# Two of four weighted one-hots compared in one VectorE instruction and weighted by ScalarE, in the scatter of a PEER layer

## The chip, the cores and the metric

The kernel runs on one core of a Trainium2 chip. A core has five engines that run beside each other, each with its own in-order queue of instructions: TensorE (PE in the profile, with PEld for its weight loads), VectorE (DVE), ScalarE (ACT), GpSimd (POOL) and SyncE (SP, which here only issues DMAs). ACT and POOL also issue DMAs from their queues. Engines wait for each other by semaphores. The metric is the time of one execution on the device in microseconds (us).

## The reference

The program is one decoder block on 1024 tokens of width 1024: RMSNorm, two gated linear recurrences (HGRN2 and GLA), an output projection, and a PEER layer, then a last RMSNorm. Only the PEER layer is touched here:

```python
q = (xb @ w_q).reshape(PEER_BLOCK, PEER_HEADS, 2, PEER_HALF)
s = jnp.einsum('thpd,hpnd->thpn', q, sub_keys)
s_top, i_top = lax.top_k(s, PEER_TOPK)
...
expert = jnp.take_along_axis(cand_idx, pos, axis=-1)
g = jax.nn.softmax(best, axis=-1)
act = jax.nn.gelu(jnp.einsum('td,thkd->thk', xb, u[expert]), approximate=False)
return jnp.einsum('thk,thkd->td', (g * act).astype(xb.dtype), v[expert])
```

Each token picks 8 x 16 = 128 experts out of 16384, numbered i * 128 + j, with a weight g each. Each expert is a row of u and a row of v.

## The kernel before

The tokens are eight tiles of 128. Two tiles (0 and 1) are done by gathering: for each of the 128 picks one indirect DMA on the POOL queue fetches a row of u (or v) per token, 512 KB in all, into a buffer `g_row`, and one VectorE instruction takes the dot product (line 833) or adds the weighted row (line 835). A third tile, tile 2, is mixed: its dot products come from gathered rows of u, its sums over v from the dense form below. The other five tiles are dense: all 128 groups of 128 experts (a group is one j) are multiplied with the tokens by TensorE. Such a dense product for one j (`DenseProducts`) loads 512 KB of u, splits it into a high and a low part (`uh` by ScalarE, `ul` by VectorE, line 84), and issues 48 matmuls 128x128 by 128x320 into `hps`. 48 is two halves of the tokens, by eight slices, by the three terms of `mm3`.

For the dense form the weights of each token have to stand at their experts' places. That is the scatter (`scatter_dense`, lines 909 to 965). For a token it makes two one-hot matrices of 128 picks by 128: `oi` for i, and `oj` for j with the weight g in the place of the one. TensorE multiplies them (`tp`, line 923), which gives the token's 128 x 128 matrix of weights, and ScalarE copies it out (`ot`, line 924). A step does four tokens, a tile has 32 steps, and six tiles give 192 steps. The buffers `oi` and `oj` hold five steps (`lag + 1`), and the matmuls of a step are issued three steps after its one-hots. The finished `ot` is stored to `gd` in DRAM by DMAs of 512 KB.

Around the scatter a planner (`Weave`) decides the order. Each piece of work says how much of each engine it takes (`Work(pe=..., dve=..., span=...)`); the planner adds these up, takes the largest sum as the time that has gone by, and whenever a filler fits under it, emits the filler. Fillers are the dense products (pe 7.2, so one for each 7.2 us of time that TensorE has not been given) and the gathered rows. The order within an engine is then settled by a scheduler. Before the sixth tile of the scatter (tile 2, the mixed one) the planner emits all gathered rows of u for that tile that are still due (`finish_mixed`); they are called the row stage below.

A dense product made in or before the scatter is spilled: its result goes to `hd` in DRAM in two stores of 160 KB (lines 884, 885) and comes back late. After the scatter four more are emitted (`EXTRA`), and one more if their number is odd. What is left is made in `experts`. In its first part (`head`, `fresh`, the head below) each j costs a dense product and the 36 matmuls 128x128 by 128x512 into `sum` and `op` that add the experts' rows of v for the six tiles. In its second part (`tail`, `stored`, the tail below) the spilled products are read back, and each j costs only the 36 matmuls. The 512 gathered rows of tiles 0 and 1 run beside these two parts, one for each 2.75 us of planned time in the head and one for each 3.75 us in the tail; what is left of them after the last j is emitted at the very end (`weave.finish(rows)`).

Of the kernel before, what the change touches and what calls it, by code (L numbers as in the profile page):

```python
# [12 lines left out]
AF = mybir.ActivationFunctionType  # L13
OP = mybir.AluOpType
# [894 lines left out]
def scatter_dense(tc, con, wk, ps, e, weights, tiles, gd, nob, lag, before, first):  # L909

    nc = tc.nc
    iota = con["iota"].unsqueeze(1).to_broadcast([P, 4, P])
    steps = TB // 4

    def cols(t, t0):
        return t[:, t0:t0 + 4].unsqueeze(2).to_broadcast([P, 4, P])

    def place(c, tb, t4, ot, oi, oj):  # L920
        pt = ps.tile([P, 4, P], F32, name="tp")
        for q in range(4):
            nc.tensor.matmul(pt[:, q], oi[:, q], oj[:, q], start=True, stop=True)  # L923
        nc.scalar.activation(ot[:, :, t4 * 4:t4 * 4 + 4], pt.rearrange("p t j -> p j t"), AF.Copy)
        if t4 == steps - 1:
            dst = gd[:, (c - NG) * (P // TB) + tb]
            q0 = first() // 16 * 16 if c == tiles[-1] and tb else 0
            for q in range(q0, q0 + P, 16):
                out.append((dst[:, q % P:q % P + 16], ot[:, q % P:q % P + 16]))

    ahead, out = [], []
    for c in tiles:
        before(c)
        ints = wk.tile([P, 2, P], I32, name="ints", bufs=1)
        nc.vector.tensor_scalar(ints[:, 0], e[:, c], 7, None, OP.arith_shift_right)
        nc.vector.tensor_scalar(ints[:, 1], e[:, c], 127, None, OP.bitwise_and)
        fl = wk.tile([P, 2, P], F32, name="fl", bufs=1)
        nc.vector.tensor_copy(fl, ints)
        tp = ps.tile([P, 4, P], F32, name="tp")
        for q, src in enumerate((fl[:, 0], fl[:, 1], weights[:, c])):  # L940
            nc.tensor.transpose(tp[:, q], src, con["ident"])
        sm = wk.tile([P, 3, P], F32, name="sm", bufs=1)
        nc.scalar.activation(sm, tp[:, 0:3], AF.Copy)
        for tb in range(P // TB):
            ot = wk.tile([P, P, TB], F32, name="ot", bufs=nob)
            for t4 in range(steps):
                t0 = tb * TB + t4 * 4
                oi = wk.tile([P, 4, P], F32, name="oi", bufs=lag + 1)
                nc.vector.tensor_tensor(oi, iota, cols(sm[:, 0], t0), OP.is_equal)
                oj = wk.tile([P, 4, P], F32, name="oj", bufs=lag + 1)  # L950
                for q in range(4):
                    t = slice(t0 + q, t0 + q + 1)
                    nc.vector.tensor_scalar(oj[:, q], con["iota"], sm[:, 1, t], sm[:, 2, t], OP.is_equal, OP.mult)  # L953
                ahead.append((c, tb, t4, ot, oi, oj))
                if len(ahead) == lag:
                    place(*ahead.pop(0))
                if out:
                    nc.scalar.dma_start(*out.pop(0))
                if c == tiles[-1] and t0 == P - 4:
                    for late in ahead:  # L960
                        place(*late)
                yield Work(pe=0.9, dve=1.35, dma=0.7, span=1.7)
    for part in out:
        nc.sync.dma_start(*part)
        yield Work(dma=1.5, span=2)
# [182 lines left out]
def block_kernel(tc, a, out):  # L1148
    nc = tc.nc
    with ExitStack() as ctx:  # L1150
# [101 lines left out]
        with ExitStack() as c1:  # L1252
            weave.run(scatter_dense(tc, con, left(c1, "sa_wk", 2), left(c1, "sa_ps", 4, space=PSUM),
                                    e, g, [*range(NG + 1, 8), NG], gd, 2, 4,
                                    lambda c: rows.finish_mixed() if c == NG else None,
                                    lambda: dense.todo[0] + EXTRA))
# [38 lines left out]
```

## Time and profile before

| | |
|---|---|
| median of 3 runs | 3400.36 us (3396.97 to 3403.42) |
| the profiled execution, its own time | 3386.81 us |
| its span, first to last instruction | 3384.8 us |
| granted TensorE clock, mean | 0.967 of full speed |
| busy: PE, DVE, POOL, ACT | 92%, 77%, 32%, 29% |
| the scatter's 192 steps on DVE | 1346.0 to 1736.3 us |

The profiled execution is 13.6 us (0.4%) faster than the median of the runs shown, so a sum made in the trace gives a difference, and this is added to the median. Matmuls are pipelined, and a busy PE is not a PE at its peak: where it matters, count the matmuls in a stretch and multiply by the distance of their starts. The same holds for the other engines: two instructions of DVE overlap by some 0.08 us, so the distance of their starts is what a step costs.

### The profile page before, as it was taken

The numbers are of one execution on the slowest core, as the hardware profiler recorded it, in microseconds if no ns is written. First come the engines' busy times: TensorE is split into PE (matmuls) and PEld (weight loads), VectorE is DVE, ScalarE is ACT, GpSimd is POOL, SyncE is SP. The second block draws the span as 40 slices with busy tenths as digits, with TensorE's granted clock in tenths as the row PEclk, the third lists the DMA queues.
The fourth block names the chain that finished last, engine by engine and source line by source line (L and its number), as shares of the span: only waits on it lengthen the run. The fifth ranks groups of instructions, "written<-read, shape, count | busy, mean of one in ns | idle before, by whom it ended". The sixth has DMA issues, their size and how long they took to land.

```text
span 3384.8 us, 47850 instructions
## 1 busy us (share of the span) xinstructions
PE 3116.0 (92%) x18146; PEld 2763.2 (82%) x18146; DVE 2598.8 (77%) x5459; ACT 977.3 (29%) x1414; POOL 1083.7 (32%) x894
## 2 busy tenths in 40 slices
PE   8988986899689998999889999999999999999996
PEld 8976776777577988999888888888888887788885
DVE  4266499848676898999777777777878877778887
ACT  4233323233232222444232222222222222233231
POOL 2001133313355243000314444444444443322322
PEclk9999997999899999999999999999999999999998
DMA  5301533334697434455858888888888788988885
GB/s 171 126 16 59 188 130 125 103 130 152 231 331 300 143 112 141 165 207 207 312 202 291 279 268 282 272 272 278 277 277 280 265 270 268 325 287 280 284 282 172
DMA packets 348392, 741.49 MB, mean 219 GB/s; under 512 B 23409, under 2 KB 195330, under 8 KB 347906
## 3 DMA queue, kind: packets, MB, share of 16 engines
q0 software_dynamic: 94464, 343.97, 29.3%
q1 hardware_dynamic: 220866, 318.82, 29.2%
q10 hardware_dynamic: 32832, 75.64, 5.8%
q8 instruction: 142, 2.33, 0.3%
q14 instruction: 88, 0.72, 0.1%
HBM read 636.50 MB, written 101.84 MB: 218 GB/s over the span
## 4 chain that ended last, share of the span: by engine, by line
PE 34%; DVE 18%; DMA 12%; issue 5%; POOL 2%; ACT 2%; SPq 0%; ACTq 0%; DVEq 0%; POOLq 0%
DMA raw<-in_c_u_t 5%; PE hps L94 4%; PE tp L923 4%; PE hps L95 4%; PE hps L96 4%; PE op L94 4%; PE op L96 3%; PE op L95 3%; DVE g_acc L835 3%; DVE g_row L833 2%; DMA raw<-hd 2%; PE sum L94 2%; PE sum L96 2%; DVE ul L84 2%; PE sum L95 2%
## 5 line engine op out<-in xcount | busy, mean ns | idle before, releaser
L801 POOL DMA_INDIRECT g_row<-in_c_u_rows,e x384 | 497.0, 1294 | 984.2 <-DVE g_row L833 837.7
L96 PE MATMUL hps<-hnTh,ul 128*128 128x320 f32 x2048 | 646.6, 316 | 25.6 <-DVE ul L84 25.6
L94 PE MATMUL hps<-hnTh,uh 128*128 128x320 f32 x2048 | 650.3, 318 | 17.0 <-ACT ht L1012 12.6
L95 PE MATMUL hps<-hnTl,uh 128*128 128x320 f32 x2048 | 645.7, 315 | 3.7 <-DVE hnTl L84 3.7
L833 DVE SCALAR_TENSOR_TENSOR g_row<-g_row,g_hn 128x1024 f32<-128x1024 f32 x384 | 463.9, 1228 | 45.4 <-DMA g_row<-in_c_u_rows,e 40.1
L801 POOL DMA_INDIRECT g_row<-in_c_v_rows,e x256 | 321.2, 1255 | 528.5 <-DVE g_acc L835 466.4
L94 PEld LDWEIGHTS hps<-hnTh,uh 128*128 128x128 f32 x2048 | 391.8, 191 | 37.4 <-ACT ht L1012 25.3
L96 PEld LDWEIGHTS hps<-hnTh,ul 128*128 128x128 f32 x2048 | 391.6, 191 | 32.8 <-DVE ul L84 28.4
L95 PEld LDWEIGHTS hps<-hnTl,uh 128*128 128x128 f32 x2048 | 391.8, 191 | 9.8 <-DVE hnTl L84 4.1
L94 PE MATMUL op<-vh,wh 128*128 128x512 f32 x768 | 307.1, 400 | 35.0 <-DVE acc L1054 34.5
L835 DVE SCALAR_TENSOR_TENSOR g_acc<-g_row,g,g_acc 128x1024 f32<-128x1024 f32 x256 | 327.7, 1280 | 8.2 <-DMA g_row<-in_c_v_rows,e 4.0
L1054 DVE TENSOR_TENSOR acc<-op,acc 128x512 f32<-128x512 f32 x330 | 225.6, 686 | 116.2 <-PE op L96 108.0
L96 PE MATMUL op<-vh,wl 128*128 128x512 f32 x768 | 303.4, 395 | 0.0
L95 PE MATMUL op<-vl,wh 128*128 128x512 f32 x768 | 302.3, 394 | 0.0
L96 PE MATMUL sum<-vh,wl 128*128 128x512 f32 x768 | 300.5, 392 | 1.2 <-DVE wl L84 1.2
L94 PE MATMUL sum<-vh,wh 128*128 128x512 f32 x768 | 299.9, 390 | 0.9 <-ACT wh L83 0.9
L95 PE MATMUL sum<-vl,wh 128*128 128x512 f32 x768 | 299.8, 390 | 0.0
L84 DVE TENSOR_TENSOR ul<-raw,uh 128x1024 fp32r<-128x1024 f32 x128 | 168.1, 1314 | 145.2 <-ACT uh L83 145.2
L83 ACT ACTIVATE uh<-raw 128x1024 fp32r<-128x1024 f32 x128 | 135.5, 1059 | 409.3 <-PE hps L95 201.2
L923 PE MATMUL tp<-oj,oi 128*128 128x128 f32 x1536 | 211.5, 278 | 4.4 <-DVE oj L953 4.2
L953 DVE TENSOR_SCALAR oj<-iota,sm 128x128 f32<-128x128 f32 x768 | 212.7, 338 | 0.0
L94 PEld LDWEIGHTS op<-vh,wh 128*128 128x128 f32 x768 | 144.9, 189 | 78.3 <-DVE acc L1054 50.8
(241 smaller groups left out, 6125.6 us busy)
## 6 DMA issues: line engine op xcount, KB each, us to landing
raw<-in_c_u_t SPq DMA_DIRECT2D x128, 512.0 KB
raw<-in_c_v_rows SPq DMA_DIRECT2D x128, 512.0 KB
gd<-ot ACTq DMA_DIRECT2D x88, 512.0 KB
w_raw<-in_w_in SPq DMA_DIRECT2D x28, 1024.0 KB
gt<-gd SPq DMA_DIRECT2D x37, 768.0 KB
gt<-gd SPq DMA_DIRECT2D x18, 1152.0 KB
hd<-ht ACTq DMA_DIRECT2D x116, 160.0 KB
raw<-hd SPq DMA_DIRECT2D x58, 320.0 KB
```

Source lines behind the costliest of these rows:

```text
L83: nc.scalar.activation(hi, src, AF.Copy)
L84: return nc.vector.tensor_sub(lo, src, hi.bitcast(F32))
L94: nc.tensor.matmul(out, l[0], r[0], start=start, stop=False)
L95: nc.tensor.matmul(out, l[0], r[1], start=False, stop=False)
L96: nc.tensor.matmul(out, l[1], r[0], start=False, stop=stop)
L801: load = nc.gpsimd.indirect_dma_start(out=row, out_offset=None, in_=self.rows[kind], in_offset=bass.IndirectOffsetOnAxis(ap=self.e[:, c, s ...
L833: nc.vector.scalar_tensor_tensor(row, row, 1.0, self.hn, OP.mult, OP.mult, accum_out=act)
L835: nc.vector.scalar_tensor_tensor(self.acc, row, w, self.acc, OP.mult, OP.add)
L923: nc.tensor.matmul(pt[:, q], oi[:, q], oj[:, q], start=True, stop=True)
L953: nc.vector.tensor_scalar(oj[:, q], con["iota"], sm[:, 1, t], sm[:, 2, t], OP.is_equal, OP.mult)
L1054: last = nc.vector.tensor_add(acc[c][:, ds], op, acc[c][:, ds])
```

## The change

Of the four weighted one-hots of a step, the first two are compared in one VectorE instruction of 128x256 without a weight (line 951 of the new kernel), and ScalarE multiplies each of the two by its weight in place (line 955). The other two are made as before (line 957). The planner's numbers for a step are lowered with it.

```diff
                 oj = wk.tile([P, 4, P], F32, name="oj", bufs=lag + 1)
+                nc.vector.tensor_tensor(oj[:, :2], iota[:, :2], cols(sm[:, 1], t0)[:, :2], OP.is_equal)
                 for q in range(4):
                     t = slice(t0 + q, t0 + q + 1)
-                    nc.vector.tensor_scalar(oj[:, q], con["iota"], sm[:, 1, t], sm[:, 2, t], OP.is_equal, OP.mult)
+                    if q < 2:
+                        nc.scalar.activation(oj[:, q], oj[:, q], AF.Copy, scale=sm[:, 2, t])
+                    else:
+                        nc.vector.tensor_scalar(oj[:, q], con["iota"], sm[:, 1, t], sm[:, 2, t],
+                                                OP.is_equal, OP.mult)
...
-                yield Work(pe=0.9, dve=1.35, dma=0.7, span=1.7)
+                yield Work(pe=0.9, dve=1.15, dma=0.7, span=1.45)
```

The lowered numbers move work that the diff doesn't name. Three places show it. First VectorE's queue, two steps in the third tile of the scatter; `iota` is the row 0 to 127, `sm` holds the picks' i, j and g:

```order
L949 TENSOR_TENSOR oi<-iota,sm 128x512
L953 TENSOR_SCALAR oj<-iota,sm 128x128 x4
L949 TENSOR_TENSOR oi<-iota,sm 128x512
L953 TENSOR_SCALAR oj<-iota,sm 128x128 x4
L949 TENSOR_TENSOR oi<-iota,sm 128x512
```

And the same with the change:

```order
L949 TENSOR_TENSOR oi<-iota,sm 128x512
L951 TENSOR_TENSOR oj<-iota,sm 128x256
L957 TENSOR_SCALAR oj<-iota,sm 128x128 x2
L949 TENSOR_TENSOR oi<-iota,sm 128x512
L951 TENSOR_TENSOR oj<-iota,sm 128x256
L957 TENSOR_SCALAR oj<-iota,sm 128x128 x2
```

A step has four instructions on VectorE in place of five, and two more on ScalarE (384 in all), which in its queue stand between the copies of `ot`.

Second SyncE's queue from the last loads of the selection (`sc`) through the scatter; `in_c_u_t` is the source of the dense products, `gd` the store of the last `ot`, `in_c_v_rows` the first load of the head. Before:

```order
L646 DMA sc<-sc_d_65 128x1024
L859 DMA raw<-in_c_u_t 128x1024 x38
L795 DMA g_hn<-hn_dram 128x1024
L859 DMA raw<-in_c_u_t 128x1024
L964 DMA gd<-ot 128x1024 x8
L1008 DMA raw<-in_c_v_rows 128x1024
L859 DMA raw<-in_c_u_t 128x1024
```

And now:

```order
L646 DMA sc<-sc_d_65 128x1024
L859 DMA raw<-in_c_u_t 128x1024 x30
L795 DMA g_hn<-hn_dram 128x1024
L859 DMA raw<-in_c_u_t 128x1024 x2
L969 DMA gd<-ot 128x1024 x8
L859 DMA raw<-in_c_u_t 128x1024
L1013 DMA raw<-in_c_v_rows 128x1024
```

Fewer dense products stand in the scatter. Counted over the whole order, 116 stores into `hd` become 104, so 58 spilled products become 52 and the head has 76 in place of 70. Up to the last `tp` matmul of the first five tiles PE has 921 matmuls into `hps` within the scatter before and 645 now; behind the last `tp` of the scatter it has 3352 before and 3720 now. VectorE splits 17 `ul` in the first five tiles before and 11 now, 7 in the row stage before and 5 now.

Third VectorE's last instructions; `g_acc<-g_row` is a gathered row, `f_ms`, `g_hn` and `raw` with a buffer's number belong to the last norm of a tile; in the new order's rows `raw` is a buffer that a j of the tail is loaded into. Before:

```order
L835 SCALAR_TENSOR_TENSOR g_acc<-g_row,g,g_acc 128x1024
L1144 SCALAR_TENSOR_TENSOR raw_29177<-acc_16349,f_rs,nf 128x1024
L72 TENSOR_SCALAR f_ms<-ss 128x1
L835 SCALAR_TENSOR_TENSOR g_acc<-g_row,g,g_acc 128x1024
L1144 SCALAR_TENSOR_TENSOR raw_29205<-acc_16350,f_rs,nf 128x1024
L835 SCALAR_TENSOR_TENSOR g_acc<-g_row,g,g_acc 128x1024
L72 TENSOR_SCALAR f_ms<-ss 128x1
L1144 SCALAR_TENSOR_TENSOR g_hn<-g_acc,f_rs,g_row 128x1024
```

And now, the last gathered row and the norm of its tile:

```order
L835 SCALAR_TENSOR_TENSOR g_acc<-g_row,g,g_acc 128x1024
L84 TENSOR_TENSOR wl<-gt,wh 128x768
L1037 TENSOR_TENSOR gt<-raw_29012,gt 128x10x64
L84 TENSOR_TENSOR vl<-raw_29064,vh 128x1024
L72 TENSOR_SCALAR f_ms<-ss 128x1
L84 TENSOR_TENSOR wl<-gt,wh 128x768
L1149 SCALAR_TENSOR_TENSOR g_hn<-g_acc,f_rs,g_row 128x1024
```

The longer head takes in more gathered rows, and the last of them stands ahead of the splits (`vl`, `wl`) of three more j, where it was the last thing but the norm before.

## Rows read from the trace of the kernel before

**Rows 1.** Busy time of every engine in seven stretches of the span: start and end, length, then PE, PEld, DVE, ACT and POOL busy us with the number of instructions, the granted clock, the DMA share and GB/s.

```profile
1346.00:1628.00 282.00, 280.68 (x2169) 276.50 (x2170) 281.38 (x825) 125.38 (x217) 0.00 (x0) 0.99 0.52 190
1628.00:1684.00 56.00, 42.99 (x276) 42.33 (x275) 35.99 (x57) 14.06 (x22) 30.80 (x23) 0.89 0.93 354
1684.00:1738.00 54.00, 51.49 (x398) 50.30 (x398) 54.00 (x163) 22.90 (x40) 1.11 (x1) 0.99 0.38 148
1840.00:2490.00 650.00, 644.26 (x3494) 570.60 (x3493) 503.45 (x785) 152.34 (x208) 286.32 (x226) 1.00 0.83 276
2490.00:2790.00 300.00, 291.50 (x1578) 257.81 (x1577) 238.84 (x259) 70.02 (x95) 142.44 (x104) 1.00 0.82 271
2940.00:3340.00 400.00, 394.75 (x1714) 320.42 (x1713) 316.82 (x337) 116.76 (x140) 117.90 (x101) 1.00 0.83 273
3340.00:3384.00 44.00, 20.20 (x87) 15.72 (x85) 30.36 (x38) 7.94 (x14) 12.61 (x12) 0.78 0.48 167
```

**Rows 2.** The same stretches, PE's matmuls into `hps` (the dense products) alone: PE busy us and their number.

```profile
1346.00:1628.00 282.00, 174.31 (x901) 0.99 0.52 190
...
2490.00:2790.00 300.00, 143.27 (x898) 1.00 0.82 271
```

**Rows 3.** The same for PE's matmuls into `op` (first two rows) and into `sum` (last two), in the late head and in the tail.

```profile
2490.00:2790.00 300.00, 87.80 (x338) 1.00 0.82 271
2940.00:3340.00 400.00, 200.02 (x851) 1.00 0.83 273
...
2490.00:2790.00 300.00, 82.67 (x342) 1.00 0.82 271
2940.00:3340.00 400.00, 199.73 (x863) 1.00 0.83 273
```

**Rows 4.** Groups of instructions from 1340 to 1740 us (the scatter): line, engine, operation, out<-in, shape, count, then busy us and mean ns of one, then the engine's idle time before them and what ended it.

```profile
L953 DVE TENSOR_SCALAR oj<-iota,sm 128x128 f32<-128x128 f32 x768 | 212.7, 338 | 0.0
...
L949 DVE TENSOR_TENSOR oi<-iota,sm 128x512 f32<-128x512 f32 x192 | 130.9, 682 | 1.6 <-ACT sm L943 1.5
...
L84 DVE TENSOR_TENSOR ul<-raw,uh 128x1024 fp32r<-128x1024 f32 x28 | 34.0, 1217 | 12.9 <-ACT uh L83 12.9
L801 POOL DMA_INDIRECT g_row<-in_c_u_rows,e x23 | 31.9, 1388 | 315.8 <-DVE g_row L833 312.4 <-issue 3.4
...
L818 DVE TENSOR_TENSOR g<-g,act 128x128 f32<-128x128 f32 x1 | 0.3, 292 | 0.4 <-ACT act L817 0.4
```

**Rows 5.** DVE in order of time, one step and the start of the next: start, length, line, operation, shape, count.

```profile
1403.50 0.69 DVE L949 TENSOR_TENSOR oi<-iota,sm 128x512 f32<-128x512 f32 x1
1404.10 1.11 DVE L953 TENSOR_SCALAR oj<-iota,sm 128x128 f32<-128x128 f32 x4
1405.13 0.69 DVE L949 TENSOR_TENSOR oi<-iota,sm 128x512 f32<-128x512 f32 x1
```

**Rows 6.** PE in order of time: 32 matmuls of `tp` and the matmul into `hps` behind them, and two neighbours within a dense product.

```profile
1400.34 3.79 PE L923 MATMUL tp<-oj,oi 128*128 128x128 f32 x32
1403.89 0.39 PE L94 MATMUL hps<-hnTh,uh 128*128 128x320 f32 x1
...
1641.04 0.31 PE L95 MATMUL hps<-hnTl,uh 128*128 128x320 f32 x1
1641.19 0.31 PE L96 MATMUL hps<-hnTh,ul 128*128 128x320 f32 x1
```

**Rows 7.** DVE in order of time: the first gathered row behind the fifth tile, the first step of the sixth tile, and the one-hots of its last step.

```profile
1628.35 1.22 DVE L833 SCALAR_TENSOR_TENSOR g_row<-g_row,g_hn 128x1024 f32<-128x1024 f32 x1
...
1684.20 0.69 DVE L949 TENSOR_TENSOR oi<-iota,sm 128x512 f32<-128x512 f32 x1
...
1735.28 1.11 DVE L953 TENSOR_SCALAR oj<-iota,sm 128x128 f32<-128x128 f32 x4
```

**Rows 8.** ACT's groups from 1340 to 1740 us, columns as in rows 4.

```profile
L924 ACT ACTIVATE ot<-tp 128x512 f32<-128x512 f32 x192 | 114.2, 598 | 153.9 <-PE tp L923 147.1 <-DMA gd<-ot 2.3 <-issue 1.2
L83 ACT ACTIVATE uh<-raw 128x1024 fp32r<-128x1024 f32 x28 | 29.5, 1054 | 29.3 <-DMA raw<-in_c_u_t 14.6 <-PE hps L95 9.6 <-DVE oi L949 2.8
L884 ACT ACTIVATE ht<-hps 128x320 f32<-128x320 f32 x57 | 24.1, 435 | 55.6 <-DMA hd<-ht 26.6 <-PE hps L96 17.2 <-DMA gd<-ot 10.3
...
L817 ACT ACTIVATE act<-act 128x128 f32<-128x128 f32 x1 | 0.3, 309 | 1.3 <-DVE g_row L833 1.3
```

**Rows 9.** Just behind the scatter, SyncE's queue and PE in order of time; the bracket is the idle time ahead and what ended it.

```profile
1737.59 6.57 SPq L964 DMA_DIRECT2D gd<-ot  x8
...
1762.00 0.64 PE L94 MATMUL hps<-hnTh,uh 128*128 128x320 f32 x1 [11.26 <-ACT ht L1012]
```

**Rows 10.** The end of the program in order of time on PE, DVE, ACT and SyncE's queue.

```profile
3361.61 0.39 PE L96 MATMUL op<-vh,wl 128*128 128x512 f32 x1
...
3362.54 0.68 DVE L1054 TENSOR_TENSOR acc<-op,acc 128x512 f32<-128x512 f32 x1
...
3377.93 1.06 ACT L1142 ACTIVATE g_hn<-g_acc 128x1024 f32<-128x1024 f32 x1 [6.41 <-DVE g_acc L835]
...
3379.93 1.28 DVE L1144 SCALAR_TENSOR_TENSOR g_hn<-g_acc,f_rs,g_row 128x1024 f32<-128x1024 f32 x1 [0.66 <-POOL f_rs L74]
...
3381.24 0.33 SPq L1145 DMA_DIRECT2D out_dram<-g_hn  x1
```

## The prediction, made before the changed kernel ran

> **What bounds the kernel now.** I read the busy time by stretches first, because the change sits in one stage and the share of a whole span says nothing about it. In the first five tiles of the scatter VectorE is busy 281.4 of 282 us and PE 280.7 of 282: both are full [rows 1]. Then comes the row stage, 56 us in which PE is busy 43.0 at a granted clock of 0.89, with the DMA engines at 93%, and then the sixth tile, in which VectorE is busy 54.0 of 54. Behind it the head and the tail, where PE is busy 97 to 99% of the time.
>
> Then one step of the scatter in order of time: a step begins 1.63 us after the one before (1403.50 to 1405.13), 0.60 of it the `oi` compare and 1.03 the four one-hots of `oj`, 0.257 each [rows 5]. 160 steps make 260.8 us, and 17 `ul` splits at 1.14 (1.217 less the overlap of 0.08) make 19.4 [rows 1, 4]: 280 of the 282 us. PE's side of the same stretch: a dense matmul starts 0.147 us after the last, and 32 matmuls of `tp` take 3.55 [rows 6]. 901 dense matmuls [rows 2] are 132 us, the `tp` of 160 steps (eight each) 142, together 274. So PE has no more than 8 us to spare there: a shorter VectorE step is worth little unless PE is given less, and that is what the planner's lowered numbers do. This is the point on which the forecast turns: dense products leave the scatter and have to be paid for in the head.
>
> **The change part by part.**
>
> First five tiles. Two one-hots go, 2 x 0.257 = 0.514 us a step. The compare of 128x256 is in no row. The nearest two are operations on two tensors, one of 128x128 at 0.292 and the `oi` compare of 128x512 at 0.682 [rows 4]; between them on a line 256 columns give 0.42, or 0.34 from start to start. The lower end is 0.21 (a 128x128 one), the upper 0.60 (a 128x512 one); I take 0.34, the point between two rows of the same kind. A step is then 0.60 + 0.34 + 0.514 = 1.456 us. 160 of them are 233, 11 `ul` splits 12.5, five tile starts 3.5: 249 us for VectorE. PE has 645 dense matmuls, 94.5 us, and the 142 of `tp`: 237. VectorE is late by 12, and where the order lumps `tp` or dense matmuls, one of the two engines waits, since only five steps of buffers lie between them; I add 6. 282 becomes 255, a gain of 27 us (23 to 33).
>
> A rule of the Trainium skill speaks against this term. Its page VectorE: DVE Perf Modes, section Walkthrough: the 8-slice pipeline in each mode, says that an fp32 operation with one tensor and scalars can use both read ports and do two elements a cycle, and that one on two tensors cannot. By streaming alone, at its 0.96 GHz, the compare would cost an estimated 0.27 us and the two operations that it replaces 0.13, a step would grow by 0.13 and the term would be a loss of 21. Here rows decide otherwise: a one-hot takes 0.257 from start to start whatever its 128 columns cost, so most of it is a fixed cost, paid once less. The side of that rule is the last rival below.
>
> ScalarE gets the two weightings. The nearest row is a 128x128 ACTIVATE, 0.309 us [rows 8]. A step is then 0.598 + 2 x 0.309 = 1.22 us of ScalarE, and the 11 products' share (1.054 + 2 x 0.435 each) 0.13 more: 1.35, under the 1.456 of VectorE. So I price it at nothing, hidden beside VectorE; without that cover it costs what is worked out under the first rival. What is queued behind a waiting weighting on ScalarE is the copy of `ot` three steps older, and PE needs that for the fourth `tp` buffer; ScalarE's idle time today, 147 us in front of `ot` for PE [rows 8], is the room.
>
> Row stage. From the first gathered row to the next step of the scatter 55.9 us pass [rows 7]. It is DMA-bound: 354 GB/s for 56 us are 19.8 MB [rows 1]. Two products fewer fall in it (249 dense matmuls were there, 135 stand there now), 2.4 of them with 0.5 MB of u and 0.3 MB of `hd` each, so 2.0 MB less, 5.6 us at the same rate; two `ul` splits fewer, for which rows had to wait, 2 to 3 us more. I take 8 (4 to 14).
>
> Sixth tile. Its 32 steps run from 1684.20 to 1736.3 [rows 7], 52.1 us, all of it VectorE. The step shrinks as before, 32 x 0.173 = 5.5 us, but PE was busy 51.5 of 54 [rows 1] and has the same products there: 3 us (0 to 5).
>
> Head and tail. 52 products are spilled in place of 58, so six j move from the tail into the head. In the late head 898 dense matmuls are 18.7 products in 300 us [rows 2] and 680 adding matmuls 18.9 j [rows 3]: 15.95 us a j. In the tail 1714 in 400 us are 47.6 j: 8.40 [rows 3]. The six cost 6 x 7.55 = 45.3 us. PE's order has 368 dense matmuls more behind the scatter, 7.67 products; the other 1.67 are spilled ones that now come just behind it, 11.8 us of PE. There PE stands idle for 11.26 us while the stores of `gd` and the first loads of the head go through [rows 9], so they may be free. Bounds: 45 and 57; I take 50.
>
> End. The last matmul ends at 3362.0 and the program 22.8 us later, because gathered rows and their norm come last [rows 10]; in the last 44 us PE is busy for 20.2 [rows 1]. With three j still to split behind the last row that tail of rows goes, and the last norm is late next: an add (0.68), the square to the end of the program from 3377.93 on (6.9), some 0.2 between: 7.8 us. Gain 15 (12 to 17).
>
> Sum against the profiled execution: -27 - 8 - 3 + 50 - 15 = -3 us, 3384 in place of 3386.8. On the median of 3400.4 that is 3397. About 0.2%, 6.8 us, is what a measurement of this kernel can tell from no change, so the forecast is no change: VectorE's time saved is handed to TensorE's queue in the head.
>
> **The rivals.**
>
> Slower: ScalarE becomes the link that ends last. Its point is a step of ScalarE above 1.456 us. For it: a weighting cannot pass a `ht` copy that waits for a store of `hd` or for PE (26.6 and 17.2 us of such waits now [rows 8]), and the one-hots of a step now go VectorE, ScalarE, PE with five buffers. Against it: the 1.35 worked out above. At the old pace of 1.63 the five tiles gain only what fewer splits give, about 7, and the sixth nothing: -7 - 8 + 50 - 15 = +20, 3420; half of that effect is 3409. The Trainium skill, page ScalarE: Activation LUTs, section What ACT_TABLE_LOAD costs, adds weight to this rival: it gives 186 ns and 0.833 per column, and 93 ns more for an operand per partition, which the weight is. That is an estimated 0.386 us in place of 0.309, and a step of ScalarE of 1.50; no row here has a per-partition scale on so small a tile.
>
> Faster: the row stage falls to what POOL needs to issue. 23 gathers at 1.388 and 0.3 between them are 39 us [rows 4], 17 less than now, and the 1.67 products are wholly free: -27 - 17 - 3 + 45 - 15 = -17, 3383. For it: fewer stores compete. Against it: the 12 MB of gathered rows (23 of 512 KB) and the stores of `gd` stay.
>
> The end gives nothing: if the rows on the chip still lag behind their place in the order, since each waits for its DMA, the last 15 us stay: +12, 3412.
>
> The compare costs as much as a 128x512 one (0.60): the step is 1.72, nothing is gained on VectorE, and 160 steps cost 14 more than before: about +30, 3430.
>
> **How the numbers follow.** The forecast has 0.52, with its own range of 3387 to 3408; the ScalarE link 0.20, the faster row stage 0.17, the end without gain 0.08, the dear compare 0.03. Within the forecast a third of its chance lies below -6.8 and a tenth above +6.8: faster 0.16, same 0.30, slower 0.06. The row stage gives 0.16 to faster; the link 0.17 to slower and 0.03 to same; the end 0.06 to slower and 0.02 to same; the compare 0.03 to slower. Sums: faster 0.32, same 0.36, slower 0.32. The range leaves out the far ends of the link and of the row stage: 3381 to 3419.
>
> **What would show it.** VectorE's step at 1.45 us with the compare near 0.42; weightings near 0.31 or 0.39 on ScalarE; first five tiles near 255 us and PE idle some 15 us more in them; the row stage near 48; some 16 us a j in the head, 8.4 in the tail; the last norm within 9 us of the last matmul. Wrong if the five tiles stay near 275 us with PE or VectorE waiting for ScalarE, if head and tail cost under 40 us more, or if a gathered row is last again.

## The result and the profile after

The changed kernel takes 3438.32 us (median of 4 runs, 3428.97 to 3450.53), against 3398.66 for the kernel before beside it on the same chip: a ratio of 1.0114, with a 95% interval of 1.0096 to 1.0132. It is slower by some 39 us. The prediction was 3397, no change, with a range of 3381 to 3419: the time lies 19 us above the range.

The profiled execution after took 3450.53 us of its own (span 3448.6), 12 us over its median, and the one before 3386.81, about 12 under its own. Of the 64 us between the two traces only some 40 are the change, so each length below is checked against other executions.

First the busy time by stretches, columns as in [rows 1]: the five tiles, the row stage, the sixth tile, the early head and, last, the end.

```profile
1351.00:1643.00 292.00, 255.72 (x1898) 251.84 (x1898) 252.63 (x665) 200.16 (x513) 3.10 (x3) 0.93 0.45 168
1643.00:1693.00 50.00, 28.77 (x168) 27.06 (x168) 30.56 (x50) 13.71 (x25) 27.08 (x21) 0.80 0.98 380
1693.00:1743.00 50.00, 47.98 (x382) 47.47 (x381) 47.95 (x129) 36.48 (x95) 0.00 (x0) 1.00 0.34 130
1850.00:2500.00 650.00, 638.04 (x3435) 564.33 (x3434) 497.38 (x774) 150.29 (x205) 282.83 (x223) 0.99 0.82 272
...
3404.00:3448.00 44.00, 32.14 (x141) 25.95 (x139) 20.05 (x30) 6.79 (x12) 3.29 (x6) 0.91 0.22 84
```

The first row is where the forecast broke. It has 1898 of PE's matmuls where before had 2169, and VectorE's shorter steps, and is longer: 292 us in place of 282. Before, PE and VectorE were both full there [rows 1]; now PE is busy for 255.7 of 292 and VectorE for 252.6, PE's granted clock is 0.93 in place of 0.99, and ScalarE is at 200, not full either. Three engines with room and a stage that got longer means that they wait for each other in turn. Who waits for whom is in the groups of these 292 us, columns as in [rows 4]; PE, VectorE, ScalarE:

```profile
L923 PE MATMUL tp<-oj,oi 128*128 128x128 f32 x1248 | 172.1, 287 | 4.4 <-ACT oj L955 4.4
L96 PE MATMUL hps<-hnTh,ul 128*128 128x320 f32 x213 | 73.2, 349 | 31.5 <-DVE ul L84 31.5
...
L949 DVE TENSOR_TENSOR oi<-iota,sm 128x512 f32<-128x512 f32 x160 | 111.2, 695 | 35.4 <-PE tp L923 31.9 <-ACT sm L943 3.1
L957 DVE TENSOR_SCALAR oj<-iota,sm 128x128 f32<-128x128 f32 x318 | 96.5, 351 | 0.0
L951 DVE TENSOR_TENSOR oj<-iota,sm 128x256 f32<-128x256 f32 x160 | 68.3, 427 | 0.0
...
L955 ACT ACTIVATE oj<-oj,sm 128x128 f32<-128x128 f32 x318 | 109.3, 393 | 21.8 <-DVE oj L951 19.1 <-DVE oi L949 1.1 <-DVE oj L957 0.9
L924 ACT ACTIVATE ot<-tp 128x512 f32<-128x512 f32 x155 | 90.6, 586 | 69.9 <-PE tp L923 69.8
```

PE waits 31.5 us for `ul`, the low parts that VectorE splits off for the dense products, and VectorE waits 31.9 us for `tp`, that is for free buffers of `oi`. Neither wait was there before: there VectorE's `oi` compares waited 1.6 us in the whole scatter, nearly all of it for `sm` [rows 4], and PE's matmuls with `ul` not at all in the same five tiles:

```profile
L96 PE MATMUL hps<-hnTh,ul 128*128 128x320 f32 x300 | 97.6, 325 | 0.0
```

PE waits for a weighting (L955) for only 4.4 us, so ScalarE is not what it waits for. The compare is 0.43 and a weighting 0.39 us.

One of these waits in order of time, on PE, VectorE and ScalarE, at the end of the second tile:

```profile
1453.63 0.30 PE L95 MATMUL hps<-hnTl,uh 128*128 128x320 f32 x1
1457.87 0.64 PE L96 MATMUL hps<-hnTh,ul 128*128 128x320 f32 x1 [3.94 <-DVE ul L84]
1458.31 0.47 PE L94 MATMUL hps<-hnTh,uh 128*128 128x320 f32 x1
1458.58 0.47 PE L95 MATMUL hps<-hnTl,uh 128*128 128x320 f32 x1
...
1451.39 0.43 DVE L951 TENSOR_TENSOR oj<-iota,sm 128x256 f32<-128x256 f32 x1
1455.14 0.69 DVE L949 TENSOR_TENSOR oi<-iota,sm 128x512 f32<-128x512 f32 x1
1456.59 1.23 DVE L84 TENSOR_TENSOR ul<-raw,uh 128x1024 fp32r<-128x1024 f32 x1
1462.02 0.29 DVE L938 CAST fl<-ints 128x256 f32<-128x256 int32 x1 [4.20 <-PE tp L941]
...
1451.57 1.06 ACT L83 ACTIVATE uh<-raw 128x1024 fp32r<-128x1024 f32 x1
...
1454.92 0.68 ACT L955 ACTIVATE oj<-oj,sm 128x128 f32<-128x128 f32 x2
```

ScalarE has `uh` ready at 1452.6, but VectorE's in-order queue has more steps of the scatter in front of the split and comes to it only at 1456.59. PE has begun the product, needs `ul` for its matmuls of L96, and stands still for 3.94 us. VectorE waits 4.20 us in its turn: its next instruction belongs to the start of a tile (L938) and needs the one buffer `fl`, which PE's transposes (L941) free, and these stand behind the wait in PE's queue. At the next product, within a tile, it is the buffers of `oi` that it waits for, 3.71 us behind a wait of PE of 4.33 us:

```profile
1484.40 0.63 PE L96 MATMUL hps<-hnTh,ul 128*128 128x320 f32 x1 [4.33 <-DVE ul L84]
...
1488.06 0.69 DVE L949 TENSOR_TENSOR oi<-iota,sm 128x512 f32<-128x512 f32 x1 [3.71 <-PE tp L923]
```

PE pays twice, since two dense matmuls start 0.27 us apart behind the wait and not 0.147 [rows 6]. PE's busy time and granted clock before the wait, in it, behind it, and when it has recovered:

```profile
1444.00:1454.00 10.00, 9.94 (x84) 1.00 0.49 195
1454.00:1458.00 4.00, 0.13 (x1) 0.89 0.19 68
1458.00:1464.00 6.00, 6.00 (x26) 0.50 0.30 87
1464.00:1474.00 10.00, 10.00 (x81) 1.00 0.47 189
```

For 6 us the clock is 0.50, the 1.2 GHz level, behind some 4 us in which PE did next to nothing.

The order of the program says why the split is late. Counted over the whole order, set beside each product the number of steps that stand on VectorE ahead of its `ul`, and the number whose `tp` stand on PE ahead of its first matmul with `ul`. Before, 16 of the 17 splits of the first five tiles stand 4 to 11 steps ahead of their use and one stands 1 step behind it. After, 9 of 11 stand 2 to 5 steps behind it, and PE waits for a split nine times in these tiles (in all, times, longest, in us):

```profile
PE hps L96 <- DVE ul L84: 31.5, 9, 5.0
```

VectorE can be five steps ahead of PE at most, as there are five buffers, so a split 5 steps late is reached only when all of them are full. That is in the order and could have been counted before the run.

The end, which answers to [rows 10]: the last matmul and the last gathered row with its norm.

```profile
3436.39 0.39 PE L96 MATMUL op<-vh,wl 128*128 128x512 f32 x1
...
3374.66 1.28 DVE L835 SCALAR_TENSOR_TENSOR g_acc<-g_row,g,g_acc 128x1024 f32<-128x1024 f32 x1
3380.07 1.29 DVE L1149 SCALAR_TENSOR_TENSOR g_hn<-g_acc,f_rs,g_row 128x1024 f32<-128x1024 f32 x1 [0.46 <-POOL f_rs L74]
```

The gathered rows are done some 73 us before the program's end, and the last matmul ends 11.9 us before it, in place of 22.8.

### The profile page after: what moved, and what is told of

It is laid out like the page before. It is cut to its first block, busy times and chain, and to the rows that moved or that the text cites. A ratio compares the mean times of both kernels' runs of the same rounds, so it can differ in the third digit from the quotient of the medians.

```text
span 3448.6 us, 48207 instructions
## 1 busy us (share of the span) xinstructions
PE 3138.0 (91%) x18146; PEld 2783.0 (81%) x18146; DVE 2573.6 (75%) x5279; ACT 1081.7 (31%) x1792; POOL 1082.8 (31%) x894
## 4 chain that ended last, share of the span: by engine, by line
PE 29%; DVE 20%; DMA 11%; issue 9%; POOL 3%; ACT 2%; SPq 0%; DVEq 0%; POOLq 0%; ACTq 0%
DMA raw<-in_c_u_t 5%; DVE g_acc L835 4%; PE hps L94 4%; PE op L94 4%; PE hps L96 3%; PE hps L95 3%; PE op L96 3%; PE op L95 3%; DVE g_row L833 3%; PE tp L923 3%; POOL g_row L801 2%; DVE ul L84 2%; DVE acc L1059 2%; DMA raw<-hd 2%; PE sum L94 2%
## 5 line engine op out<-in xcount | busy, mean ns | idle before, releaser
L96 PE MATMUL hps<-hnTh,ul 128*128 128x320 f32 x2048 | 651.2, 319 | 51.9 <-DVE ul L84 51.9
L96 PEld LDWEIGHTS hps<-hnTh,ul 128*128 128x128 f32 x2048 | 394.7, 193 | 62.5 <-DVE ul L84 57.8
L94 PE MATMUL op<-vh,wh 128*128 128x512 f32 x768 | 307.4, 400 | 49.6 <-DVE acc L1059 49.2
L96 PE MATMUL op<-vh,wl 128*128 128x512 f32 x768 | 304.4, 396 | 0.0
L96 PE MATMUL sum<-vh,wl 128*128 128x512 f32 x768 | 301.3, 393 | 0.0
L83 ACT ACTIVATE uh<-raw 128x1024 fp32r<-128x1024 f32 x128 | 135.5, 1058 | 435.9 <-PE hps L95 254.2
L1017 ACT ACTIVATE ht<-hps 128x320 f32<-128x320 f32 x152 | 65.8, 433 | 472.3 <-PE hps L96 468.3
```

Source lines behind the costliest of these rows:

```text
L83: nc.scalar.activation(hi, src, AF.Copy)
L94: nc.tensor.matmul(out, l[0], r[0], start=start, stop=False)
L96: nc.tensor.matmul(out, l[1], r[0], start=False, stop=stop)
L1017: nc.scalar.activation(ht, hps, AF.Gelu)
```

## The experiments

Three theories stood at the start. **S**: late splits. **N**: the planner's lowered numbers, by giving PE slack and the head six more j. **L**: ScalarE's weightings as a link. The first four runs are a square: new or old instructions, new or old numbers, and the new instructions with a rule that brings the splits forward. Each ratio is to the kernel before, run beside it.

**New instructions, old numbers.**

```diff
-                yield Work(pe=0.9, dve=1.15, dma=0.7, span=1.45)
+                yield Work(pe=0.9, dve=1.35, dma=0.7, span=1.7)
```

> The new instructions with the planner's old numbers (1.35, 1.7), so again 58 spilled products and nothing moved into the head. Theory S (late splits: in the new order each split `ul` of a dense product stands on VectorE 3 to 5 steps behind the place at which PE asks for it, PE waits for it, its clock falls, VectorE then waits for PE): the order with these numbers still has 15 of 17 splits of the first five tiles behind PE's place, so these tiles take longer than before, 295 to 320 us against 282, with over 30 us of PE waiting for `ul`, and the time is 3405 to 3435. Theory N (the lowered numbers alone did it, by giving PE slack and the head six more j): the time is at or under that of before, 3385 to 3400. Theory L (ScalarE's weightings are a link that ends last at 1.8 us a step): first five tiles about 291 us as with the change, and with nothing moved into the head about 3408, PE waiting for ScalarE and not for `ul`.

3435.91 us (ratio 1.0106, 1.0076 to 1.0136). N fell as the whole cause: with the old numbers, and nothing moved into the head, it is as slow as the change. S has it nearly right: the first five tiles took 318.4 us, the time is 1 us above its range, and PE's wait is 26.6 us where over 30 were expected. Their stretch, and the waits in it:

```profile
1348.00:1665.00 317.00, 289.25 (x2167) 286.49 (x2168) 256.34 (x667) 209.58 (x528) 0.00 (x0) 0.95 0.45 166
...
L96 PE MATMUL hps<-hnTh,ul 128*128 128x320 f32 x297 | 97.8, 334 | 26.6 <-DVE ul L84 26.6
...
L949 DVE TENSOR_TENSOR oi<-iota,sm 128x512 f32<-128x512 f32 x160 | 110.0, 687 | 53.2 <-PE tp L923 49.7 <-ACT sm L943 3.5
```

In this order 14 of 17 splits are late by 1 to 5 steps. So it is the new instructions, not the numbers, with which the scheduler settled on late splits; why it places them so is not shown.

**Old instructions, new numbers.** The same line the other way round, in the kernel before.

> The old instructions with the planner's new numbers (1.15, 1.45), so 52 spilled products and six j more in the head, as with the change. S: the order has nearly all splits at or ahead of PE's place, so PE hardly waits for `ul` in the first five tiles, and VectorE is full: 160 steps of 1.63, 11 splits of 1.14 and 3.5 us of tile starts are 277 us; with the row stage at -6, the end at -15 and the head and tail at +50 to +65 the time is 3422 to 3440. N: first five tiles about 291 us with PE waiting for `ul` as with the change, 3438 to 3450. L: as S. What head and tail cost more than before is the price of the six j by itself.

3429.95 us (1.0096, 1.0058 to 1.0134), the first five tiles 274.6 us: VectorE full, as S and L had it. One split of 11 is late here.

```profile
1347.00:1621.00 274.00, 255.40 (x1929) 245.65 (x1929) 273.77 (x817) 117.16 (x202) 0.00 (x0) 0.99 0.48 179
...
L96 PE MATMUL hps<-hnTh,ul 128*128 128x320 f32 x218 | 71.6, 334 | 6.0 <-DVE ul L84 6.0
```

The numbers alone cost 32 us too, but elsewhere: from the end of the scatter to the last matmul this run takes 1695.8 us, against 1625.6 before. That is the price of the six j in the head and some of the difference between executions; the averages below part the two.

**The splits brought forward** to two steps behind the product's place in the program, in the changed kernel.

```diff
+            self.splits.append([2, self.options[0].last])
...
-                nc.vector.tensor_tensor(oi, iota, cols(sm[:, 0], t0), OP.is_equal)
+                cmp = nc.vector.tensor_tensor(oi, iota, cols(sm[:, 0], t0), OP.is_equal)
+                for late in [x for x in dense.splits if x[0] == 0]:
+                    tc.add_manual_dep(cmp.ins, late[1].ins.name, nosync(), reason="split first")
+                dense.splits = [[n - 1, x] for n, x in dense.splits if n]
```

> The changed kernel with one rule more for the order: VectorE's compare two steps behind a product's place in the program has to stand behind that product's split, so the splits stand 2 steps behind PE's place and not 4 or 5; nothing else is asked. S: PE's wait for `ul` in the first five tiles falls from 31.5 us to under 10, its clock is back at 0.97 or more there, these tiles take 255 to 268 us in place of 291, and the time is 3402 to 3416 against 3438 with the change. L: ScalarE does as much as before, the tiles stay at 285 to 291 us and the time at 3432 to 3440. N: as L.

3426.65 us (1.0086, 1.0056 to 1.0117), the first five tiles 280.9: some 12 us better, where S expected 23 to 36 (255 to 268 in place of 291). PE's wait fell only to 23.6 us:

```profile
L96 PE MATMUL hps<-hnTh,ul 128*128 128x320 f32 x213 | 71.3, 340 | 23.6 <-DVE ul L84 23.6
```

Two steps late (9 of the 11 splits) is still late. The likely reason is that PE, with little to do between products, runs close behind VectorE. And `uh` itself stands on ScalarE only three `ot` ahead of its use in this order, so the split could not go much further forward by this rule.

**The same rule with the old numbers.**

> The new instructions, the old numbers and the same rule for the splits. S: the first five tiles are bound by PE, whose 901 products' matmuls and 160 steps of `tp` are 274 us: 274 to 284 us, nothing is moved into the head, and the time is 3388 to 3402. L: 291 us or more in these tiles, 3405 or more. N: as S.

3422.92 us (1.0067, 1.0046 to 1.0088), the first five tiles 304.3 where S had 274 to 284. PE still waits 18.2 us for `ul`. At this point S had the sign right twice and the size wrong twice. In the changed order PE's products also stand in lumps: behind 37 steps nine matmuls or more, behind 52 none (before: 22 and 35). Hence a fourth theory, **U**: the lumps.

**Products dealt out evenly**: four matmuls behind each step's `tp`, by order alone. With it PE takes a product at its place in the program, two products later than the scheduler had pulled it forward, so the splits are also 16 to 23 steps early (the last one 3).

```diff
-            nc.tensor.matmul(pt[:, q], oi[:, q], oj[:, q], start=True, stop=True)
+            m = nc.tensor.matmul(pt[:, q], oi[:, q], oj[:, q], start=True, stop=True)
+            if q == 0 and behind:
+                tc.add_manual_dep(m.ins, behind.pop().ins.name, nosync(), reason="even")
+        credit[0] += 4.0
+        got = dense.step(m, int(credit[0]))
+        credit[0] -= int(credit[0])
+        if got:
+            behind[:] = [got]
...
+    def step(self, tp, n):
+        last = None
+        while self.open and n >= 1:
+            last = self.waiting
+            if tp is not None:
+                self.tc.add_manual_dep(last.ins, tp.ins.name, nosync(), reason="even")
+            self.waiting = next(self.open, None)
...
```

> The changed kernel with the matmuls of the dense products dealt out evenly in the first five tiles: four of them behind each step's `tp` in PE's order, in place of twelve behind some steps and none behind others. With it the splits stand 16 to 23 steps ahead of PE's place. Theory U (uneven products: where twelve stand behind a step it takes PE 0.94 + 12 x 0.147 = 2.7 us and VectorE waits for buffers, where none stand PE is done in 0.94 and waits for VectorE): VectorE is left as the only bound, 160 steps of 1.456, 11 splits of 1.14 and 3.5 us of tile starts: 249 to 262 us for the first five tiles against 292 with the change, granted clock 0.97 or more there, and 3400 to 3414 for the whole (1.4 products, some 10 us of PE, move behind the fifth tile and may not all be hidden there). Theory L (ScalarE's weightings in the chain VectorE, ScalarE, PE set the pace): 280 to 291 us and 3426 to 3440. Theory S (late splits alone): as with the early split, 281 us and about 3427.

3399.19 us (1.0005, 0.9992 to 1.0018): the whole loss is gone. The first five tiles take 250.1 us. Their stretch, PE's split matmul (L877 in this kernel), VectorE's compare of `oi` and ScalarE's weighting:

```profile
1348.00:1598.00 250.00, 242.57 (x1862) 234.10 (x1862) 248.38 (x663) 202.92 (x514) 2.01 (x2) 0.98 0.52 194
...
L877 PE MATMUL hps<-hnTh,ul 128*128 128x320 f32 x192 | 63.1, 328 | 0.0
...
L987 DVE TENSOR_TENSOR oi<-iota,sm 128x512 f32<-128x512 f32 x160 | 109.5, 685 | 2.4 <-ACT sm L981 2.4
...
L993 ACT ACTIVATE oj<-oj,sm 128x128 f32<-128x128 f32 x318 | 110.7, 395 | 43.7 <-DVE oj L989 37.9 <-DVE oj L995 4.4
```

VectorE is busy 248.4 of 250, PE waits for no split, and ScalarE does the same weightings at the same 0.39 us and waits 42 us for VectorE between them. PE does wait 10.4 us for weightings here, more than with the change, but no `oi` compare waits for PE, so it does not hold VectorE up:

```profile
L951 PE MATMUL tp<-oj,oi 128*128 128x128 f32 x1272 | 175.3, 283 | 12.1 <-ACT oj L993 10.4 <-ACT ot L959 0.7
```

L falls: a link that ended last in the changed kernel would have done so here.

**Twelve matmuls behind each of four steps, none behind the next nine**, the splits 19 to 24 steps early for 8 of the 11 products (33, 15 and 3 for the others). This tells lumps from late splits.

```diff
-        credit[0] += 4.0
+        credit[0] += 12.0
```

> As the run with evenly dealt products, but twelve matmuls behind each of four steps' `tp` and none behind the next nine, which is as lumped as the changed kernel's own order or more; the splits stand 19 to 24 steps ahead of PE's place. It tells the two parts of the cause apart. If lumps alone cost the time (theory U): 275 to 292 us for the first five tiles and 3424 to 3440. If they cost it only together with the late splits (theory S+U: a lump of 48 matmuls and four `tp` takes PE 10.6 us, in which VectorE makes 7.3 steps, and the buffers let it be three to four steps ahead of where it is when it follows closely, so that it hardly waits; but when the lump begins with a wait for a split that stands 5 steps late, VectorE is at the end of its buffers already): 250 to 264 us and 3398 to 3412.

3405.76 us (1.0026, 1.0011 to 1.0040), the first five tiles 254.2:

```profile
1351.00:1604.00 253.00, 244.22 (x1868) 237.47 (x1869) 249.41 (x664) 201.16 (x513) 2.51 (x2) 0.99 0.52 193
...
L987 DVE TENSOR_TENSOR oi<-iota,sm 128x512 f32<-128x512 f32 x160 | 108.5, 678 | 3.0 <-ACT sm L981 2.5 <-PE tp L951 0.5
```

Lumps as heavy as the scheduler's cost 4 us in these tiles while the splits are early: VectorE waits 0.5 us for PE. So U alone falls, and S stands, joined with the lumps: 38 of the changed kernel's 292 us go away with the late splits, though the lumps stay. Even dealing with splits five steps late wasn't tried, so what late splits cost without lumps is not shown.

**Even products with the old numbers**, 5.6 matmuls a step, new instructions.

> The new instructions, the planner's old numbers and the products dealt out evenly, five or six matmuls a step. U: PE is the bound in the first five tiles, 840 matmuls of products at 0.147 and 160 steps of `tp` at 0.89, 266 us: 266 to 276 us against 318 with the same numbers and the scheduler's own order; nothing is moved into the head, and the time is 3386 to 3402, within 0.3% of before. L: 285 us or more, 3405 or more.

3387.16 us (0.9966, 0.9952 to 0.9979): faster than both kernels. The first five tiles take 267.8 us, bound by PE:

```profile
1352.00:1619.00 267.00, 265.14 (x2092) 264.59 (x2093) 254.32 (x667) 211.83 (x529) 0.00 (x0) 0.99 0.54 198
```

**The kernel before with even products** is the control for this.

> The kernel before, its instructions and numbers, with the products dealt out evenly. It tells what even dealing gives without the change. VectorE is full there with 160 steps of 1.63 and 16 or 17 splits: 277 to 282 us for the first five tiles, so nothing is gained, 3394 to 3402, and the 12 us of the run with new instructions and old numbers are the change's own gain. If the even order by itself is what made that run faster (a steadier clock, or PE's work moved into the row stage): 3384 to 3390.

3399.36 us (1.0002, 0.9990 to 1.0014), the first five tiles 282.6. Even dealing gives nothing to the old instructions, so the 12 us are what the new ones are worth once their order is right.

**Gathered rows placed closer**, alone in the kernel before, and on top of the even products with the old numbers.

```diff
-PACE = (2.4, 14.0, 2.75, 3.75)
+PACE = (2.4, 14.0, 2.7, 3.7)
```

> The kernel before with the gathered rows of tiles 0 and 1 placed a little closer (2.7 and 3.7 us of planned time each in place of 2.75 and 3.75), so that the last of them stands well ahead of the last j. It measures the term of the end by itself: if the end gives what was forecast, the program ends about 8 us behind the last matmul in place of 22.8, and the time falls by 12 to 17 us, to 3381 to 3387. If the rows on the chip lag behind their place or cost PE time elsewhere, it falls by less than 5 us.

> The edits of the two runs above together. If they add up: 3371 to 3387, faster than before by 0.3 to 0.8%. L: 3390 or more.

Alone: 3395.83 us, a ratio of 0.9997 (0.9983 to 1.0010). Together: 3384.34 (0.9959, 0.9941 to 0.9977), the fastest here, though 3 us under the run without it is within the noise. In both traces the last matmul ends 11.8 us before the end of the span, so the stretch at the end gives its 11 us, and the time does not show them. From the end of the scatter to the last matmul these two take 1642.5 and 1643.7 us, and the five other executions with 58 spilled products 1635.1 on average (1625.6 to 1642.9). Rows that come earlier may cost PE those 8 us; with one of the five at 1642.9 that is not shown.

**The change once more**, for a second trace.

> The changed kernel once more, for a second execution's profile. First five tiles 288 to 295 us, PE waiting some 30 us in them for `ul`, the end 11 to 12 us behind the last matmul, 3430 to 3450. If the first profile was an odd one, these tiles differ by over 8 us.

3438.47 us (1.0117, 1.0085 to 1.0148). The first five tiles take 292.3 us, with 32.4 us of PE waiting for `ul`: the first trace was no odd one there.

The stages of the runs, in us, each from one execution. The five tiles run from the first `oi` compare to the first gathered row behind the fifth tile, the sixth to the end of its last one-hots, head and tail from there to the end of the last matmul:

| | five tiles | row stage | sixth tile | head and tail | end |
|---|---|---|---|---|---|
| before | 282.3 | 55.9 | 52.2 | 1625.6 | 22.8 |
| the change | 292.5 | 49.2 | 50.6 | 1693.3 | 11.9 |
| the change once more | 292.3 | 49.6 | 50.3 | 1686.5 | 11.9 |
| new instructions, old numbers | 318.4 | 55.2 | 54.0 | 1638.6 | 22.9 |
| old instructions, new numbers | 274.6 | 43.1 | 53.9 | 1695.8 | 11.9 |
| early splits | 280.9 | 48.3 | 50.3 | 1683.5 | 11.9 |
| early splits, old numbers | 304.3 | 54.4 | 51.1 | 1633.7 | 23.3 |
| even products | 250.1 | 46.6 | 53.5 | 1679.8 | 11.9 |
| even products, old numbers | 267.8 | 55.5 | 53.7 | 1634.5 | 22.6 |
| lumps, early splits | 254.2 | 49.7 | 51.3 | 1681.1 | 11.9 |
| before, even products | 282.6 | 52.3 | 52.2 | 1642.9 | 22.6 |
| before, rows closer | 282.3 | 55.6 | 52.2 | 1642.5 | 11.8 |
| even products, old numbers, rows closer | 267.3 | 54.9 | 53.8 | 1643.7 | 11.8 |

## Why the prediction was wrong

The failed step is the first five tiles: "VectorE is late by 12, and where the order lumps `tp` or dense matmuls, one of the two engines waits [...]; I add 6. 282 becomes 255". They became 292. The 249 us of VectorE's work in that sentence's sum were right: the run with even products takes 250.1. The add-on of 6 was mis-sized: it is 43. It stood for lumps, which with early splits cost 4, and it left out the splits' places in VectorE's queue. The prediction counted how many `ul` were left, 11, and not where they stand. It treated the freed time of PE as room, and PE spent it waiting for splits. The freed time is not what puts the splits late: with the old numbers, which leave PE its products, 14 of 17 stand late too.

The other terms, by the step:

- **The compare** was taken at 0.34 from start to start and is 0.34 (the step is 1.45 in every trace with the new instructions). The dear compare is out. By streaming alone the Trainium skill (VectorE: DVE Perf Modes, Walkthrough: the 8-slice pipeline in each mode) would have it at an estimated 0.27; the rows have more, and the step shrank all the same.
- **ScalarE priced at nothing** was right, but for the wrong price: a weighting is 0.393, not 0.309. The Trainium skill (ScalarE: Activation LUTs, What ACT_TABLE_LOAD costs) makes it an estimated 0.386 by its figure for an operand per partition, and the trace agrees. With 0.393 a step of ScalarE comes to 1.5 us by the prediction's own sum, no less than VectorE's. But that sum adds lengths, and instructions of ScalarE overlap: two weightings in a row take 0.68 us together (in the rows of the wait above), so 0.29 from start to start, and ScalarE is busy for 202.9 us in the run with even products, 1.27 a step. This is under VectorE's 1.45, the weightings wait 42 us for VectorE there, and the link does not end last. The first rival had the right side (3420), by a mechanism that the runs contradict.
- **Row stage** -8: measured -6.5 (mean of the two traces). **Sixth tile** -3: measured -1.7. Both within their bounds.
- **Head and tail** +50 (45 to 57): the five executions with 58 spilled products and the planner's old rows average 1635.1, the six with 52 average 1686.7: +51.6. Of the five, the profiled execution of before is the shortest, by 8 us, which would be most of why it lies under its own median. PE's wait of 11.26 us behind the scatter [rows 9] is 1.01 in the trace after, so the spilled products that come there were partly free, as allowed for.
- **End** -15 (12 to 17): the stretch gives 10.9, just outside the bounds, as the last norms end 11.9 us and not 7.8 behind the last matmul. The runs with closer rows leave open whether even that reaches the time.

With the measured terms the sum is +10 - 6.5 - 1.7 + 51.6 - 10.9 = +42.5, and the medians differ by 40: nothing large is left over. Had the splits been early, it would have been about 0, which is what the forecast said and the run with even products measured.

## What to carry to other kernels

Where a scheduler settles the order, a changed instruction on one engine can move instructions that the diff doesn't name. Before summing durations, put two queues of the new order side by side and count, for each value that one hands the other, how many steps its producer stands ahead of its consumer; a producer that stands behind its consumer's place makes the consumer wait, here already at two steps with five buffers between the engines, and when the buffers are full both wait. And time taken from one engine is worth what the engine that is full beside it can use: here 12 us, with the products left in the scatter and dealt out evenly, and nothing with six of them moved into the head.

## What was not expected of the hardware

A wait costs PE more than its length. Behind 4 us with almost no matmul the granted clock stood at 0.50, the 1.2 GHz level, for the next 6 us, in which it did 26 matmuls, while 81 took 10 us once it was back at 1.00. Over the five tiles the clock was 0.93 in the changed kernel and 0.98 to 0.99 in the two runs with its numbers and splits many steps early.

Executions whose head and tail hold the same products differ there by up to 16 us (1679.8 to 1695.8 us over six executions of five kernels), and two executions of the changed kernel by 7, as much as most terms of the sum: one trace against another does not settle a term of that size there, so averages over several runs were compared.
